# One encoder layer on one core: the first stage in an order fixed by hand, half as many sines, and Hyena's projection begun in its tail

## The chip, the cores and the metric

The kernel runs on one core of a Trainium2 chip. The metric is device time in microseconds (us) of one execution; the median of three runs is shown. A profiled execution gives the trace from which all rows below are read. The engines are TensorE (PE in the rows, its weight loads PEld), VectorE (DVE), ScalarE (ACT), GpSimd (POOL) and SyncE (SP). Transfers are issued by SyncE, by ScalarE or by GpSimd; a trailing q (SPq, ACTq) marks the issuing of a transfer.

## The reference, cut to what matters

One layer of an encoder over 2048 tokens of width 1024, in 32-bit floats. The first product's columns go to attention (8 query heads, 2 key heads and 2 value heads of 64) and to Hyena (`u`, 1536 columns):

```python
a = rms_norm(h, norm1_g[i])
q, k, v, u = jnp.split(a @ w_in[i], [512, 640, 768], axis=-1)
q = apply_axial_rope(rms_norm(q, q_norm_g[i]), *tables)
k = apply_axial_rope(rms_norm(k, k_norm_g[i]), *tables)
att = block_attention(q, k, v)                 # softmax over all 2048 keys
hy = hyena_mixer(u, ...)                       # short conv of u, then two long convolutions by FFT
```

Hyena's filters come from a small network over the 2048 positions, evaluated for all positions in both directions:

```python
z = jnp.concatenate([t, jnp.cos(ang), -jnp.sin(ang)], axis=-1)      # 2048 x 33
h = jnp.sin(freq * (z @ w1 + b1))
h = jnp.sin(freq * (h @ w2 + b2))
h = jnp.sin(freq * (h @ w3 + b3))
h = (h @ w4) * jnp.exp(-t * jnp.abs(deltas))
fwd, bwd = h[:, :, 0], h[:, :, 1]                                   # bwd enters reversed
```

Behind this come the Fourier transforms of filters and signal, the mix of both heads with an output projection, and a squared-ReLU MLP.

## The kernel before

Products of 32-bit accuracy are made from three matmuls of split operands, `high x high`, `high x low`, `low x high` (`mm3`, lines 162 to 166). Every operand is therefore split into a high part (ScalarE, a rounding copy) and a low part (VectorE, a subtraction).

**First stage** (`qkv_proj`, line 172). Sixteen tiles of 128 tokens. For each tile: load `xt`; ScalarE squares and sums it, takes a square root, scales (`xs`, lines 204, 116, 206); TensorE transposes it in eight pieces (`tp`, line 215); ScalarE and VectorE split it (`ah`, `al`, lines 217 and 218); both parts go to DRAM as `aT_d`. Then 24 matmuls of 512 columns make q and 24 of 256 columns make k and v (`qkv<-wh,ah` and its two companions). ScalarE copies and squares the result (`y`, `z`, `v`), GpSimd multiplies by gains and cosines, VectorE makes norms and the rotation, the result is split (`hl`, `kk`), transposed (`tq`, line 279), copied (`qs`, line 281) and stored. The weights `wh` and `wl` are split at the start from eight raw rows of 512 and eight of 256 columns (lines 189 to 193, raw tiles `wraw`, two buffers each).

Beside it `filter_hidden` (line 1226) goes on by a step a tile: the three sine layers, in 16 arguments of 512 columns (a matmul `fo` and seven VectorE instructions each, lines 1213 to 1219) and 16 sines on ScalarE (line 1250). Its small weights are loaded by SyncE.

In this stage a list scheduler sets the order of instructions on each engine: an instruction that is ready may go ahead of an earlier one that waits.

**Attention** (`attention`, line 445) runs 512 steps, each a score block of 128 keys by 512 queries, and begins with 22 more that make only the peaks of scores (`sc`, `top`, AHEAD = 22). Side work goes along: a generator is pumped once a step. Its first 16 steps make filter taps (`filter_taps`, `ft`, `taps`), then one step of taps alternates with six of `u_proj` (line 330), Hyena's projection: 48 column tiles (four blocks of 512 tokens by 12 tiles of 128 columns) of 24 matmuls `uo<-aT,uw` each, from the stored `aT_d` and from raw weights `uraw` that are split in the first block. What the side generator has left over at the end of attention runs off alone. The small tables `cw`, `cb` (short convolution), `dl` and `skip` are loaded by SyncE where they are used, their elements far apart in DRAM (lines 336, 339, 1294, 1302). Attention's softmax weights are `p` (line 484). The next stage begins with `fs` (line 1482).

Of the kernel before, what the change touches and what calls it, by code (L numbers as in the profile page):

```python
# [11 lines left out]
F32 = mybir.dt.float32  # L12
# [33 lines left out]
def setup(tc, ctx, a):  # L46
# [10 lines left out]
    aligned(k.cpool, 64)  # L57
# [104 lines left out]
def mm3(k, out, l_hi, l_lo, r_hi, r_lo, start, stop):  # L162
    mm = k.nc.tensor.matmul
    mm(out, l_hi, r_hi, start=start, stop=False)  # L164
    mm(out, l_hi, r_lo, start=False, stop=False)  # L165
    mm(out, l_lo, r_hi, start=False, stop=stop)  # L166


XL, FL = 1, 3


def qkv_proj(k, pa, ps, side):
# [12 lines left out]
    wh = pa.tile([P, ND, W], F32R, name="wh", bufs=1)  # L185
    wl = pa.tile([P, ND, W], F32R, name="wl", bufs=1)

    def load_w(c0, c1):
        for d in range(ND):
            raw = pa.tile([P, c1 - c0], F32, name=f"wraw{c0}", bufs=2)  # L190
            nc.sync.dma_start(out=raw[:], in_=w_in[d * P:(d + 1) * P, c0:c1])
            nc.scalar.mul(out=wh[:, d, c0:c1], in_=raw[:], mul=k.g1[:, d:d + 1])
            nc.vector.scalar_tensor_tensor(out=wl[:, d, c0:c1], in0=raw[:], scalar=k.g1[:, d:d + 1],
                                           in1=f32(wh[:, d, c0:c1]), op0=ALU.mult, op1=ALU.subtract)

    def load_x(t):
        xt = pa.tile([P, DM], F32, name="xt", bufs=2)
        nc.sync.dma_start(out=xt[:], in_=x[t * P:(t + 1) * P, :])
        return xt

    def normed(t, xt):
        xs = pa.tile([P, DM], F32, name="xs", bufs=XL + 1)
        ssq = pa.tile([P, 1], F32, name="ssq")
        nc.scalar.activation(out=xs[:], in_=xt[:], func=AF.Square, accum_out=ssq[:])
        r = rstd_from_root(k, pa, ssq[:], DM, 1, "rstd")
        nc.scalar.mul(out=xs[:], in_=xt[:], mul=r[:])
        return xs

    def turned(t, xs):
        hi = pa.tile([P, ND, P], F32R, name="ah", bufs=2)  # L210
        lo = pa.tile([P, ND, P], F32R, name="al", bufs=2)
        for d0 in range(0, ND, 4):
            tp = ps.get("tp", "tp")
            for d in range(4):
                nc.tensor.transpose(tp[:, d * P:(d + 1) * P], xs[:, (d0 + d) * P:(d0 + d + 1) * P], k.ident[:])
            c = tp[:].rearrange("p (d t) -> p d t", t=P)
            nc.scalar.copy(out=hi[:, d0:d0 + 4], in_=c)
            nc.vector.tensor_sub(out=lo[:, d0:d0 + 4], in0=c, in1=f32(hi[:, d0:d0 + 4]))
        for i, part in enumerate((hi, lo)):
            nc.sync.dma_start(out=k.aT_d[i, :, t * P:(t + 1) * P].rearrange("(d p) t -> p d t", p=P), in_=f32(part[:]))  # L220
        return hi, lo

    def project(hi, lo, c0, cw):
# [5 lines left out]
    NH = NQ + NKV  # L229

    def taken(t, oq, okv):
        y = pa.tile([P, NH, HD], F32, name="y", bufs=2)
        nc.scalar.copy(out=y[:, :NQ], in_=oq[:].rearrange("p (h e) -> p h e", e=HD))
        nc.scalar.copy(out=y[:, NQ:], in_=okv[:, :P].rearrange("p (h e) -> p h e", e=HD))
        v = pa.tile([P, NKV, HD], F32, name="v")
        nc.scalar.copy(out=v[:], in_=okv[:, P:2 * P].rearrange("p (h e) -> p h e", e=HD))
        nc.sync.dma_start(out=k.v_d[t], in_=v[:])
        z = pa.tile([P, NH, HD], F32, name="z", bufs=2)
        nc.scalar.activation(out=z[:, :NQ], in_=oq[:].rearrange("p (h e) -> p h e", e=HD), func=AF.Square)
        nc.scalar.activation(out=z[:, NQ:], in_=okv[:, :P].rearrange("p (h e) -> p h e", e=HD), func=AF.Square)  # L240
        cs = pa.tile([P, 2, HD], F32, name="cs", bufs=2)
        nc.sync.dma_start(out=cs[:], in_=a["rope"][t * P:(t + 1) * P])
        for i, s in enumerate((slice(0, NQ), slice(NQ, NH))):
            n = s.stop - s.start
            nc.gpsimd.tensor_mul(out=y[:, s], in0=y[:, s], in1=qkg[:, i:i + 1].to_broadcast([P, n, HD]))
        w = pa.tile([P, NH, HD], F32, name="w", bufs=2)
        nc.gpsimd.tensor_mul(out=w[:], in0=y[:], in1=cs[:, 0:1].to_broadcast([P, NH, HD]))
        return y, z, w, cs

    def norm_rope(t, y, z, w, cs):  # L250
        ss = pa.tile([P, NH], F32, name="ss")
        nc.vector.tensor_reduce(out=ss[:], in_=z[:], axis=AX.X, op=ALU.add)
        r = rstd_from_root(k, pa, ss[:], HD, NH, "qr")
        yv = y[:].rearrange("p h (a b e) -> p h a b e", a=2, b=2)
        zv = z[:].rearrange("p h (a b e) -> p h a b e", a=2, b=2)
        sv = cs[:, 1].rearrange("p (a b e) -> p a b e", a=2, b=2)
        for ax in range(2):
            for b in range(2):
                nc.vector.tensor_mul(out=zv[:, :, ax, b], in0=yv[:, :, ax, 1 - b],
                                     in1=sv[:, ax, b].unsqueeze(1).to_broadcast([P, NH, 16]))  # L260
        nc.vector.tensor_add(out=w[:], in0=w[:], in1=z[:])
        nc.vector.tensor_mul(out=w[:], in0=w[:], in1=r[:].unsqueeze(2).to_broadcast([P, NH, HD]))
        hl = pa.tile([P, NH, 2, HD], F32R, name="hl", bufs=FL)
        nc.scalar.copy(out=hl[:, :, 0], in_=w[:])
        nc.vector.tensor_sub(out=hl[:, :, 1], in0=w[:], in1=f32(hl[:, :, 0]))
        return hl

    def twice(hl):
        kk = pa.tile([P, NKV, 2, 2, HD], F32R, name="kk", bufs=FL - 1)
        nc.gpsimd.tensor_copy(out=kk[:, :, :, 0], in_=f32(hl[:, NQ:]))  # L270
        nc.gpsimd.tensor_copy(out=kk[:, :, 0, 1], in_=f32(hl[:, NQ:, 0]))
        nc.gpsimd.tensor_copy(out=kk[:, :, 1, 1], in_=unit[:].unsqueeze(1).to_broadcast([P, NKV, HD]))
        return hl, kk

    def finish(t, hl, kk, g):
        tp = ps.get("tq", "tq", F32R)
# [12 lines left out]
    xt, xs, aT, yz, hl = {}, {}, {}, {}, {}  # L289
    xt[0] = load_x(0)  # L290
    load_w(0, QW)
    xt[1] = load_x(1)
    load_w(QW, W)
    qkg = pa.tile([P, 2, HD], F32, name="qkg", bufs=1)
    nc.sync.dma_start(out=qkg[:, 0], in_=a["q_norm_g"].to_broadcast([P, HD]))
    nc.sync.dma_start(out=qkg[:, 1], in_=a["k_norm_g"].to_broadcast([P, HD]))
    nc.vector.tensor_scalar_mul(out=qkg[:, 0], in0=qkg[:, 0], scalar1=HD ** -0.5)
    oq = {}
    for i in range(-1 - XL, NT + FL):
        if i == 13:  # L300
            k.first = load_q(k, 0), {(0, b): load_k(k, k.early, 0, b, 4) for b in range(2)}, load_v(k, k.early, 0)
        if 1 < i + XL + 2 < NT:
            xt[i + XL + 2] = load_x(i + XL + 2)
        e = i - FL
        ending = 0 <= e < NT
        if ending:
            finish(e, *hl[e], 0)
        if 1 < i < NT:
            oq[i] = project(*aT[i], 0, QW)
        if ending:  # L310
            finish(e, *hl[e], 1)
        if 0 <= i + 1 < NT:
            aT[i + 1] = turned(i + 1, xs.pop(i + 1))
        if 0 <= i + XL + 1 < NT:
            xs[i + XL + 1] = normed(i + XL + 1, xt.pop(i + XL + 1))
        if 0 <= i + 1 < 2:
            oq[i + 1] = project(*aT[i + 1], 0, QW)
        pump(side, 1 if i > 0 else 0)
        if ending:
            finish(e, *hl.pop(e), 2)  # L320
        if 0 <= i < NT:
            okv = project(*aT.pop(i), QW, 256)
        if 0 <= i - 1 < NT:
            hl[i - 1] = twice(norm_rope(i - 1, *yz.pop(i - 1)))
# [1495 lines left out]
```

## Time and profile before

| | |
|---|---|
| median of three runs | 3129.85 us (3125.67 to 3130.92) |
| profiled execution | 3129.86 us |
| its span, first to last instruction | 3127.9 us |
| mean granted clock of TensorE | 0.980 of full speed |
| busy: TensorE, VectorE, GpSimd, ScalarE | 95%, 65%, 55%, 45% of the span |
| last product of the first stage, first `p`, next stage's first matmul | 208.0, 268.8, 1219.0 us |

Busy time counts the stretches in which an engine executes something. A granted clock of 1.00 is the upper of TensorE's two levels, 2.4 GHz, and 0.50 the lower, 1.2 GHz; matmuls overlap at their ends, so a matmul's own duration is longer than the distance to the next. Idle time of an engine names the instruction that ended it. An engine with a low share of the span can still be the one that is waited for in a stretch.

### The profile page before, as it was taken

The numbers are of one execution on the slowest core, as the hardware profiler recorded it, in microseconds if no ns is written. First come the engines' busy times: TensorE is split into PE (matmuls) and PEld (weight loads), VectorE is DVE, ScalarE is ACT, GpSimd is POOL, SyncE is SP. The second block draws the span as 40 slices with busy tenths as digits, with TensorE's granted clock in tenths as the row PEclk, the third lists the DMA queues.
The fourth block names the chain that finished last, engine by engine and source line by source line (L and its number), as shares of the span: only waits on it lengthen the run. The fifth ranks groups of instructions, "written<-read, shape, count | busy, mean of one in ns | idle before, by whom it ended". The sixth has DMA issues, their size and how long they took to land.

```text
span 3127.9 us, 40514 instructions
## 1 busy us (share of the span) xinstructions
PE 2985.5 (95%) x13400; PEld 2247.5 (72%) x13400; DVE 2047.3 (65%) x3157; ACT 1421.5 (45%) x2626; POOL 1717.1 (55%) x1395
## 2 busy tenths in 40 slices
PE   8978999999999998999999989999999899999998
PEld 6755666666666666676667768887888778888887
DVE  7987776666666654777465567777977554454455
ACT  7866655555555444444444563333333233223333
POOL 3434777777778885244555327777877553250010
PEclk9988999999999999999999999999999999999999
DMA  7758344333424525776656794445544393433454
GB/s 225 223 155 241 113 130 137 113 112 121 151 96 119 157 91 163 267 251 213 188 174 196 253 310 160 160 155 192 188 158 150 137 358 120 138 108 134 147 182 150
DMA packets 482461, 534.44 MB, mean 171 GB/s; under 512 B 49604, under 2 KB 344004, under 8 KB 475212
## 3 DMA queue, kind: packets, MB, share of 16 engines
q1 hardware_dynamic: 463708, 511.59, 50.3%
q0 software_dynamic: 4480, 14.68, 1.3%
q10 hardware_dynamic: 14064, 5.58, 0.7%
q8 instruction: 107, 1.75, 0.2%
q14 instruction: 102, 0.84, 0.1%
HBM read 326.22 MB, written 198.19 MB: 168 GB/s over the span
## 4 chain that ended last, share of the span: by engine, by line
PE 41%; DMA 3%; POOL 2%; issue 2%; ACT 1%; DVE 1%; ACTq 0%; SPq 0%; POOLq 0%; DVEq 0%
PE y L164 7%; PE y L165 7%; PE y L166 7%; PE g L166 5%; PE g L165 5%; PE g L164 5%; PE X L1451 1%; PE b L1582 1%; DMA ml<-sb 1%; PE yo L1647 1%; PE op L166 0%; PE op L164 0%; POOL r L956 0%; PE op L165 0%; ACT sb L793 0%
## 5 line engine op out<-in xcount | busy, mean ns | idle before, releaser
L489 POOL TENSOR_TENSOR sum<-sum,p 128x512 f32<-128x512 f32 x416 | 553.1, 1329 | 120.6 <-ACT p L484 94.8
L464 DVE TENSOR_REDUCE top<-sc 128x1 f32<-128x512 f32 x512 | 346.9, 686 | 252.3 <-PE sc L461 249.2
L484 ACT ACTIVATE p<-st 128x512 f32<-128x512 f32 x512 | 303.1, 597 | 302.2 <-PE st L482 285.3
L164 PE MATMUL g<-mh,wop 128*128 128x512 f32 x896 | 350.7, 391 | 5.7 <-ACT wop L922 5.4
L166 PE MATMUL g<-mh,wop 128*128 128x512 f32 x896 | 350.8, 391 | 2.4 <-DVE wop L923 2.4
L165 PE MATMUL g<-ml,wop 128*128 128x512 f32 x896 | 350.8, 392 | 2.2 <-DVE ml L933 2.2
L164 PE MATMUL y<-bh,ah 128*128 128x512 f32 x768 | 300.0, 391 | 12.4 <-ACT ah L1127 12.4
L1106 DVE TENSOR_TENSOR ah<-ar,ah 128x1024 fp32r<-128x1024 f32 x111 | 150.1, 1353 | 229.7 <-ACT ah L1105 227.2
L165 PE MATMUL y<-bh,ah 128*128 128x512 f32 x768 | 299.8, 390 | 0.0
L166 PE MATMUL y<-bh,ah 128*128 128x512 f32 x768 | 299.8, 390 | 0.0
L1105 ACT CAST ah<-ar 128x1024 fp32r<-128x1024 f32 x111 | 117.1, 1055 | 345.6 <-PE y L166 334.0
L502 PE MATMUL o<-p,vt 128*64 128x512 f32 x1024 | 234.9, 599 | 0.0
L461 PE MATMUL sc<-kt,q 128*128 128x512 f32 x512 | 208.5, 412 | 13.4 <-DVE top L464 11.6
L481 PE MATMUL st<-q,kt 128*128 128x512 f32 x512 | 214.5, 419 | 1.3 <-ACT p L484 1.2
L482 PE MATMUL st<-q,kt 128*128 128x512 f32 x512 | 203.1, 397 | 0.0
L164 PEld LDWEIGHTS g<-mh,wop 128*128 128x128 f32 x896 | 169.3, 189 | 41.8 <-ACT wop L922 6.0
L166 PEld LDWEIGHTS g<-mh,wop 128*128 128x128 f32 x896 | 169.4, 189 | 38.3 <-DVE wop L923 3.3
L165 PEld LDWEIGHTS g<-ml,wop 128*128 128x128 f32 x896 | 169.2, 189 | 38.4 <-DVE ml L933 3.3
L922 ACT CAST wop<-ws 128x512 fp32r<-128x512 f32 x128 | 79.3, 621 | 231.2 <-PE g L166 173.6
L164 PEld LDWEIGHTS y<-bh,ah 128*128 128x128 f32 x768 | 144.8, 188 | 43.0 <-ACT ah L1127 12.9
L165 PEld LDWEIGHTS y<-bh,ah 128*128 128x128 f32 x768 | 144.6, 188 | 30.4 <-DVE bh L1098 0.3
L166 PEld LDWEIGHTS y<-bh,ah 128*128 128x128 f32 x768 | 144.6, 188 | 30.1 <-DVE ah L1128 0.3
(303 smaller groups left out, 7050.4 us busy)
## 6 DMA issues: line engine op xcount, KB each, us to landing
ar<-H_d SPq DMA_DIRECT2D x109, 512.0 KB, 3.8
uw<-uw_d SPq DMA_DIRECT2D x36, 1024.0 KB, 5.0
w1raw<-in_w_mlp_in SPq DMA_DIRECT2D x64, 512.0 KB, 4.3
H_d<-r SPq DMA_DIRECT2D x96, 256.0 KB, 2.2
H_d<-s SPq DMA_DIRECT2D x96, 256.0 KB, 2.0
F_d<-F SPq DMA_DIRECT2D x34, 512.0 KB, 3.4
F<-F_d SPq DMA_DIRECT2D x34, 512.0 KB, 3.9
aT<-aT_d SPq DMA_DIRECT2D x32, 512.0 KB, 6.0
```

The costliest lines, as they stand in the source:

```text
L164: mm(out, l_hi, r_hi, start=start, stop=False)
L165: mm(out, l_hi, r_lo, start=False, stop=False)
L166: mm(out, l_lo, r_hi, start=False, stop=stop)
L461: nc.tensor.matmul(s[:], u.q[:, h], kt[u.kv, b][0][:], start=True, stop=True)
L464: k.mark_v = nc.vector.tensor_reduce(out=u.top[:, h, b:b + 1], in_=s[:], axis=AX.X, op=ALU.max, negate=True)
L481: nc.tensor.matmul(s[:], lo[:, c], u.q2[:].rearrange("p h t -> p (h t)"), start=True, stop=False)
L482: nc.tensor.matmul(s[:], hi[:, c], u.q[:].rearrange("p h t -> p (h t)"), start=False, stop=True)
L484: nc.scalar.activation(out=p[:], in_=s[:], func=AF.Exp)
L489: k.mark = nc.gpsimd.tensor_add(out=u.sum[:], in0=u.p0[:] if j == 1 else u.sum[:], in1=p[:])
L502: nc.tensor.matmul(u.o[cols], vt[j // 8][:, j % 8, u.kv], p[:], start=j < 2, stop=j > 13)
L1105: nc.scalar.copy(out=h[:, 0], in_=raw[:])
L1106: nc.vector.tensor_sub(out=h[:, 1], in0=raw[:], in1=f32(h[:, 0]))
```

## The change

1. **Order.** The whole first stage and the first steps of `u_proj` stand in a block in which TensorE, VectorE, ScalarE and GpSimd execute in the order in which the code is written (`in_order`); only SyncE's order is still the scheduler's. The loop over tiles is rewritten so that its parts stand in the order wanted. The weights' raw tiles get three buffers (q) and four (k, v).
2. **Sines.** The two halves of the 2048 positions are stacked on the partitions (before: the two directions), so that the inner layers are computed once for both directions: 8 arguments instead of 16. The second direction is the first, reversed by GpSimd copies. The frequency is divided by 2 pi once, so that an argument is three VectorE instructions and ScalarE scales by 2 pi within the sine.
3. **Hyena's projection** starts in the first stage: raw weights of column tile 0 from tile 11 on, its splits at tiles 12 to 14, its 24 matmuls between the last turns, and START = 30 more steps (column tiles 1 to 3) ahead of attention, where it was 0. The eight `aT` tiles lie in the space that `wh`, `wl` and `xt` leave, so their loads wait for the last product.
4. **Small loads.** `cw`, `cb`, `dl`, `skip`, the q and k gains, the 16 filter weights and biases and the two tiles `z` are issued by GpSimd instead of SyncE.

```diff
-    for i in range(-1 - XL, NT + FL):
+    for i in range(-3, NT + 2):
...
+        if own:
+            oq = project(i, *q_cols)
+        if 0 <= i - 1 < NT:
+            rot = rotation(i - 1)
+            next(rot)
...
+        if own:
+            okv[i] = project(i, *kv_cols)
+        if i > 0:
+            pump(side)
+        pump(u, {NT - 5: 1, NT - 4: 3, NT - 3: 3, NT - 2: 3}.get(i, 0))
+        if i == NT - 1:
+            pw_pool.__exit__(None, None, None)
+            pump(u)
...
     nc.vector.tensor_scalar(out=x[:], in0=ps, scalar1=bias, scalar2=freq, op0=ALU.add, op1=ALU.mult)
-    nc.vector.tensor_scalar(out=n[:], in0=x[:], scalar1=1.0 / (2.0 * math.pi), scalar2=MAGIC,
-                            op0=ALU.mult, op1=ALU.add)
-    nc.vector.tensor_scalar(out=n[:], in0=n[:], scalar1=MAGIC, scalar2=None, op0=ALU.subtract)
-    for c in TWO_PI:
-        nc.vector.scalar_tensor_tensor(out=x[:], in0=n[:], scalar=-c, in1=x[:], op0=ALU.mult, op1=ALU.add)
-    nc.vector.tensor_scalar(out=x[:], in0=x[:], scalar1=PI_IN, scalar2=-PI_IN, op0=ALU.min, op1=ALU.max)
+    nc.vector.tensor_scalar(out=n[:], in0=x[:], scalar1=MAGIC, scalar2=MAGIC, op0=ALU.add, op1=ALU.subtract)
+    nc.vector.tensor_sub(out=x[:], in0=x[:], in1=n[:])
...
-            nc.sync.dma_start(out=w3[h, i, j * H:(j + 1) * H], in_=a["filt_w3"][0])
+            nc.gpsimd.dma_start(out=w3[h, i, j * H:(j + 1) * H], in_=a["filt_w3"][0])
...
+    nc.vector.tensor_scalar_mul(out=fr[:], in0=fr[:], scalar1=1.0 / (2.0 * math.pi))
...
-    for b in range(4):
+    for b in range(2):
...
+        src = f32(k.hc[:, 0, max(p0, 1):p0 + 512])[:, ::-1]
+        nc.gpsimd.tensor_copy(out=k.hc[:, 1, SEQ - p0 - 511:SEQ - max(p0, 1) + 1], in_=src)
...
-START = 0
+START = 30
...
+            with sbuf(k, "uf") as k.uf:
+                k.u, k.u_tag, k.calm = u_proj(k), "qk", True
+                with sbuf(k, "p1", 2, side="right") as p1, sbuf(k, "f1", side="right") as f1:
+                    with Banks(k, "ps1", {"tp": 2, "qk": 3, "tq": 2, "fl": 1}) as k.ps, in_order(tc):
+                        qkv_proj(k, p1, k.ps, filter_hidden(k, f1, k.ps), k.u)
+                        k.calm = False
+                        pump(k.u, START)
```

What this moves is seen in each engine's order of instructions. GpSimd's, between the work on q of tile 1 and on k and v of tile 1 (`w_471` to `w_473` are the filter's weights, `fb` and `fr` its biases and frequencies; in brackets the counters that an instruction waits for); before:

```order
L245 TENSOR_TENSOR y<-y,qkg 128x512 [waits DVE_49,Activation_49]
L245 TENSOR_TENSOR y<-y,qkg 128x512 [waits Activation_49]
L245 TENSOR_TENSOR y<-y,qkg 128x128 [waits DMAHW2_49,Activation_49]
L247 TENSOR_TENSOR w<-y,cs 128x640 [waits DMAHW3_49,Pool_49]
L245 TENSOR_TENSOR y<-y,qkg 128x128 [waits Activation_49]
L271 CAST kk<-hl 128x2x64 [waits Activation_49]
```

now:

```order
L1328 DMA fr<-in_filt_freq 64x1 [waits DMASW5_49]
L1322 DMA w_471<-in_filt_w 33x64 [waits DMASW6_49]
L1323 DMA w_472<-in_filt_w 64x64 [waits DMASW7_49]
L1325 DMA w_473<-in_filt_w 64x64 [waits DMASW0_49]
L1325 DMA w_473<-in_filt_w 64x64 [waits DMASW1_49]
L1327 DMA fb<-in_filt_b 64x1 [waits DMASW2_49]
L1327 DMA fb<-in_filt_b 64x1 [waits DMASW3_49]
L1327 DMA fb<-in_filt_b 64x1 [waits DMASW4_49]
L1328 DMA fr<-in_filt_freq 64x1 [waits DMASW5_49]
L274 TENSOR_TENSOR y<-y,qkg 128x128 [waits Activation_49]
L280 TENSOR_TENSOR w<-y,cs 128x640 [waits DMAHW4_49,Pool_49]
```

These are the last nine of sixteen loads that stand between two steps of the rotation where there were none; each waits for a counter of the queue that an earlier load raises, and the work on tile 1 (`y`, `w`) follows behind them.

VectorE's, between the low parts `al` of tile 2 and the rotation of tile 1 (`ss` is the sum of squares of the heads, `qry`, `qre`, `qr` the steps to its inverse root); before, at the first rotation:

```order
L121 SCALAR_TENSOR_TENSOR rstd<-rstde,rstd 128x1 [waits DVE_49]
L252 TENSOR_REDUCE ss<-z 128x10 [waits Activation_49]
L218 TENSOR_TENSOR al<-tp,ah 128x512 [waits DMAHW4_49,Activation_49]
L218 TENSOR_TENSOR al<-tp,ah 128x512 [waits Activation_49]
L114 TENSOR_SCALAR qry<-ss 128x10 [waits DVE_49]
L259 TENSOR_TENSOR z<-y,cs 128x10x16 [waits Pool_49]
L259 TENSOR_TENSOR z<-y,cs 128x10x16
L118 RECIPROCAL qr<-qre 128x10 [waits Activation_49]
```

now:

```order
L304 TENSOR_TENSOR hl<-w,hl 128x10x64 [waits Activation_49]
L249 TENSOR_TENSOR al<-tp,ah 128x512 [waits Activation_49] x2
L1329 TENSOR_SCALAR fr<-fr 128x1 [waits DMASW5_49]
L285 TENSOR_REDUCE ss<-z 128x10 [waits Activation_49]
L118 TENSOR_SCALAR qry<-ss 128x10 [waits DVE_49]
L294 TENSOR_TENSOR z<-y,cs 128x10x32 [waits Pool_49]
L294 TENSOR_TENSOR z<-y,cs 128x10x32
L122 RECIPROCAL qr<-qre 128x10 [waits Activation_49]
```

The new row is the division of `fr`, which waits for a load that GpSimd issued.

TensorE's, behind the last product of the first stage (`hl` and `kk` are what `tq` transposes, `fo` is a product of the filter's layers, `uo` one of Hyena's projection); before:

```order
L164 MATMUL qkv<-wh,ah 128x256
L165 MATMUL qkv<-wl,ah 128x256
L166 MATMUL qkv<-wh,al 128x256
L279 MATMUL tq<-identr,hl 128x128 [waits DVE_49,Activation_49]
L279 MATMUL tq<-identr,hl 128x128 x3
L279 MATMUL tq<-identr,hl 128x128 [waits Activation_49]
L279 MATMUL tq<-identr,hl 128x128 x3
L1255 MATMUL fo<-sx,w_387 128x512 [waits DVE_49]
L279 MATMUL tq<-identr,kk 128x128 [waits Activation_49,Pool_49]
L279 MATMUL tq<-identr,kk 128x128 x3
```

now:

```order
L169 MATMUL qkv<-wl,ah 128x256
L170 MATMUL qkv<-wh,al 128x256
L316 MATMUL tq<-identr,hl 128x128 [waits DVE_49,Activation_49]
L316 MATMUL tq<-identr,hl 128x128 x3
L168 MATMUL uo<-aT,uw_2006 128x512 [waits DMAHW0_49]
L169 MATMUL uo<-aT,uw_2006 128x512
L170 MATMUL uo<-aT,uw_2006 128x512
L168 MATMUL uo<-aT,uw_2006 128x512 [waits DMAHW1_49]
L169 MATMUL uo<-aT,uw_2006 128x512
L170 MATMUL uo<-aT,uw_2006 128x512
L316 MATMUL tq<-identr,hl 128x128 [waits Activation_49]
L316 MATMUL tq<-identr,hl 128x128 x3
```

Between the turns of the last two tiles now stand matmuls of the projection, each group of three waiting for the load of one `aT` tile; the filter's products stand earlier.

## Rows read from the trace of the kernel before

**Rows 1.** Page, busy time of each engine, share of the span, instructions.
```profile
PE 2985.5 (95%) x13400; PEld 2247.5 (72%) x13400; DVE 2047.3 (65%) x3157; ACT 1421.5 (45%) x2626; POOL 1717.1 (55%) x1395
```

**Rows 2.** Stretches: length; busy time by engine; granted clock; share of transfer engines; GB/s.
```profile
core 0: us, PE busy (x) PEld busy (x) DVE busy (x) ACT busy (x) POOL busy (x), PEclk, DMA share, GB/s
13.00:31.50 18.50, 17.93 (x84) 14.16 (x83) 10.07 (x29) 14.31 (x27) 2.59 (x2) 1.00 0.93 284
31.50:208.00 176.50, 165.25 (x992) 137.61 (x990) 162.21 (x362) 134.99 (x257) 74.91 (x84) 0.98 0.68 202
208.00:270.00 62.00, 33.34 (x90) 18.84 (x90) 45.24 (x95) 34.26 (x72) 7.10 (x9) 0.61 0.74 181
270.00:544.00 274.00, 260.33 (x1106) 171.49 (x1104) 204.83 (x345) 162.52 (x342) 198.09 (x150) 0.98 0.46 145
544.00:1194.00 650.00, 649.46 (x2876) 431.64 (x2875) 400.41 (x613) 337.01 (x603) 526.19 (x399) 1.00 0.37 119
1194.00:1219.00 25.00, 23.08 (x104) 16.48 (x103) 3.84 (x11) 4.22 (x7) 5.24 (x5) 1.00 0.59 143
```

**Rows 3.** Time line of TensorE: start, length, instruction, count, idle time before.
```profile
26.07 0.39 PE L164 MATMUL qkv<-wh,ah 128*128 128x512 f32 x1
26.30 0.39 PE L165 MATMUL qkv<-wl,ah 128*128 128x512 f32 x1
...
31.31 1.03 PE L215 MATMUL tp<-ident,xs 128*128 128x128 f32 x8
...
203.90 1.09 PE L1255 MATMUL fo<-sx,w 128*128 128x512 f32 x2
...
207.95 0.28 PE L166 MATMUL qkv<-wh,al 128*128 128x256 f32 x1
...
228.44 1.61 PE L461 MATMUL sc<-kt,q 128*128 128x512 f32 x3
232.81 0.79 PE L461 MATMUL sc<-kt,q 128*128 128x512 f32 x1 [2.76 <-DVE top L464]
237.05 1.48 PE L461 MATMUL sc<-kt,q 128*128 128x512 f32 x2 [3.44 <-DVE top L464]
...
247.79 1.39 PE L461 MATMUL sc<-kt,q 128*128 128x512 f32 x2 [5.08 <-DVE top L464]
...
1219.03 1.05 PE L1482 MATMUL fs<-table,e 128*128 128x128 f32 x8
```

**Rows 4.** Groups by form on VectorE, 0 to 230 us: busy, mean ns.
```profile
L1218 DVE SCALAR_TENSOR_TENSOR sx<-sn,sx 128x512 f32<-128x512 f32 x32 | 28.1, 878 | 0.3
```

**Rows 5.** Transfers issued in the first 275 us: count, size, us to landing.
```profile
wraw<-in_w_in SPq DMA_DIRECT2D x8, 128.0 KB, 3.5
...
uraw<-in_w_in SPq DMA_DIRECT2D x2, 512.0 KB, 8.3
...
w<-in_filt_w SPq DMA_DIRECT2D x6, 16.0 KB, 3.3
```

**Rows 6.** Time line of ScalarE.
```profile
16.28 1.06 ACT L204 ACTIVATE xs<-xt 128x1024 f32<-128x1024 f32 x1 [1.97 <-DMA xt<-in_x]
...
18.96 1.14 ACT L206 ACTIVATE xs<-xt,rstd 128x1024 f32<-128x1024 f32 x1
...
22.86 2.33 ACT L192 ACTIVATE wh<-wraw,g 128x512 fp32r<-128x512 f32 x4
...
268.76 0.60 ACT L484 ACTIVATE p<-st 128x512 f32<-128x512 f32 x1 [0.99 <-PE st L482]
```

**Rows 7.** Line 800's instructions: GpSimd issuing a transfer, ns min/median/max.
```profile
L800 POOL DMA_DIRECT2D ml<-sb x20: 536/536/538, 1778.4 to 1828.8; - x20
```

**Rows 8.** Time line of SyncE's queue.
```profile
231.00 3.45 SPq L1302 DMA_DIRECT2D skip<-in_hy_skip_d  x1
...
241.95 6.44 SPq L339 DMA_DIRECT2D cb<-in_hy_conv_b  x1
```

**Rows 9.** Time line of GpSimd.
```profile
26.72 1.29 POOL L245 TENSOR_TENSOR y<-y,qkg 128x512 f32<-128x512 f32 x1 [24.56 <-ACT y L233]
```

More of the change, by code (lines that the diff above doesn't have):

```diff
@@ L227, in project @@
         return o
[L229 to L248, printed above, removed]
@@ L268, in twice, with heads @@
[L268 to L276, printed above, removed]
+    def heads(o, n):
+        return o[:, :n * HD].rearrange("p (h e) -> p h e", e=HD)
@@ new lines, in qkv_proj @@
+    xt, xs, rs, aT, y, z, w, cs, hl, kk, tq, okv = ({} for _ in range(12))
+    q_cols, kv_cols = (0, QW), (QW, W)
+    load_x(0)
+    for d in range(4):
+        load_w(d, *q_cols)
+    load_x(1)
+    for d in range(4, ND):
+        load_w(d, *q_cols)
+    for d in range(4):
+        load_w(d, *kv_cols)
+    load_x(2)
+    for d in range(4, ND):
+        load_w(d, *kv_cols)
+    nc.gpsimd.dma_start(out=qkg[:, 0], in_=a["q_norm_g"].to_broadcast([P, HD]))
+    nc.gpsimd.dma_start(out=qkg[:, 1], in_=a["k_norm_g"].to_broadcast([P, HD]))
@@ new lines, in qkv_proj @@
+    k.qkg = qkg
+    small_tables(k)
+    ahead = {-2: range(4), -1: range(4, ND)}
+    for i in range(-3, NT + 2):
+        norms = rot = iter(())
+        own, mine = 0 <= i < NT, 0 <= i - 2 < NT
+        tail = i >= NT
+        if 2 < i + 5 < NT:
+            load_x(i + 5)
+        if i == NT - 3:
+            k.first = load_q(k, 0), {(0, b): load_k(k, k.early, 0, b, 4) for b in range(2)}, load_v(k, k.early, 0)
+        if mine:
+            turn(i - 2, 0)
+        if tail:
+            pump(u, 2)
+        if 0 <= i - 1 < NT:
+            taken(i - 1, okv.pop(i - 1), 1)
+        if mine:
+            stored(i - 2, 0)
+        if own:
[3 more added lines that the diff above has]
+            next(rot)
+        if 0 <= i + 2 < NT:
+            scaled(i + 2)
+        if i == -2:
+            turned(0)
+            turned_low(0)
+        for d in ahead.get(i, ()):
+            split_w(d, *q_cols)
+        pump(rot)
+        if 0 <= i + 3 < NT:
+            norms = squared(i + 3)
+            pump(norms, 2)
+        pump(rot)
+        pump(norms)
+        if mine:
+            turn(i - 2, 1)
+        if tail:
+            pump(u, 2)
+        pump(rot)
+        if mine:
+            stored(i - 2, 1)
+        if 0 < i + 1 < NT:
+            turned(i + 1)
+        pump(rot)
+        if 0 < i + 1 < NT:
+            turned_low(i + 1)
+        if i == 0:
+            for d in range(ND):
+                split_w(d, *kv_cols)
+        if mine:
+            turn(i - 2, 2)
+        if own:
+            taken(i, oq, 0)
+        if mine:
+            stored(i - 2, 2)
+        if own:
+            okv[i] = project(i, *kv_cols)
+            del aT[i]
+        if i > 0:
[4 more added lines that the diff above has]
+            pump(u)
```

289 lines of the change are left out of this document (156 added, 133 removed).

## The prediction

> **What bounds the kernel now.** I read the busy shares first, then stretches of the first 1219 us, then groups of instructions, then the time lines at the seams. TensorE is busy in 2985.5 of 3127.9 us [rows 1], so only its 142 us of gaps, its slow-clock stretches and whatever work is taken off it can pay. The stretches show where the change can reach [rows 2]. From 31.5 to 208 us (the products of the token tiles) TensorE is busy 165.25 of 176.5 us, so 11.25 us are gaps, and VectorE is busy 162.21: the two bind together. From 208 to 270 TensorE is busy only 33.3 of 62 us, at a mean granted clock of 0.61, that is, for most of it at the lower of its two levels (1.2 of 2.4 GHz). From 270 to 544 it is busy 260.3 of 274, and from 544 to 1194 it is full (649.46 of 650) at clock 1.00. From 1194 to 1219 the last products of Hyena's projection run with almost nothing of attention beside them. Behind 1219 the code is the same, so I take that part over at its present length and predict one number: when the stage that now starts at 1219.03 [rows 3] will start.
>
> **Sines.** Before there were 16 arguments, now 8, each with one `fo` product of two records, which keep TensorE busy for 1.09 us [rows 3], some 1.0 beyond what overlaps. Thirteen of the 16 fall before 208 us: 13 us of the 165.25 go and 8 come back. On VectorE seven instructions an argument become three; the two dearest, of 0.88 us each [rows 4], are among those that go, so 32 x 0.88 = 28 us at least leave an engine that was busy for 162 of 176.5. VectorE stops being a bound in that stretch, and its gaps no longer explain TensorE's. Fewer table loads on ScalarE lay beside TensorE's products; I give them nothing.
>
> **The start.** Before, TensorE takes products of q0, q1 and kv0 as weights arrive: at 31.31 us all 72 are through and the next transposes begin [rows 3]. In the fixed order it runs q0, then kv0, then q1, each complete. kv0's last four weight rows are loaded into the buffers of its first four, so SyncE's issue waits until VectorE has split those; such a load lands after 3.5 us [rows 5]. The split stands on ScalarE behind four squares, three scalings, two pairs of `ah` and eight parts of q: by its rows 4 x 1.25, 3 x 1.14 and, at 0.58 each (four in 2.33 us), twelve more, 15.4 us [rows 6], from 5 us on without any wait for a load. So kv's splits begin at 21 to 23 and its last at 31 to 34. I get q0 at 25 to 27, kv0 at 37 to 39, and q1 5.5 us later (24 x 0.23, the distance from one wide product to the next [rows 3]), or up to 49 where the slow clock comes in: all 72 at 45, against 31.3. That is a loss of 13.7, with 10 and 17.7 as its ends.
>
> **The rest of the first stage.** TensorE's work behind those 72 is 165.25 - 13 + 8 = 160.2 us. To it come waits that the fixed order makes.
> (a) VectorE's `fr<-fr` stands between the low parts of tile 2 and the sum of squares of tile 1, and needs the sixteenth of the filter loads, which POOL issues behind `y` of q1. POOL issues a load in 0.536 us [rows 7], each of the last eight waits for the one eight earlier, and SyncE's loads of this kind landed after 3.3 us [rows 5]: 8.6 us if no wait bites, plus one landing, 11.9. Everything behind it on VectorE waits, and through it ScalarE and, once q2 and kv1 are through, TensorE. I take 9, ends 4 and 20 (two landings of some 6 us beside the issues).
> (b) `z` is one more POOL load for each half of the filter's positions, and TensorE's `fo` waits for it in its queue: an issue and a landing, 0.5 + 3.3, I take 4, ends 0 and 6.
> (c) Three batches of sines stand on ScalarE ahead of the copy of kv, and the next layer's products wait for them in TensorE's queue. No row shows such a wait; its ends are nothing and, three times, two products as long as a pair of records (1.09 us [rows 3]), 6.5. I take 4.
> (d) Of today's 11.25 us of gaps I keep 2, at the turns, ends 0 and 3.
> Together 19, ends 6 and 35. The last product then ends at 45 + 160.2 + 19 = 224 (before 208).
>
> The four small tables (4608 + 1536 + 2048 + 1024 elements of four bytes) go to POOL's queue as well. Bounds: 4 x 0.54 = 2.2 us [rows 7]; or, at the 6.44 us for which the issue of the 1536 elements of `cb` holds SyncE's queue [rows 8], 4.2 ns each, 39 us. POOL has no tile work before 26.72 us [rows 9] and none that TensorE waits for before about 40, so the upper end costs 0 to 3 us; I take 0. SyncE gains: `skip` (3.45 us) and `cb` no longer hold it at 231 and 242 [rows 8], where the loads of `aT` stood behind.
>
> The Trainium skill (DMA: Bandwidth & Descriptors, "Anatomy of one DMA — SWDGE (gpsimd) path") fits a POOL-issued transfer by a fixed 2.0 us plus its bytes. The trace shows 0.536 us of POOL for one and no small load among them; if the 2.0 us were paid one after the other, sixteen would take 32 us, and (a) would be some 29 instead of 9.
>
> **The tail.** Before, from the last product (207.95 [rows 3]) to the first weight `p` of attention (268.76 [rows 6]) pass 60.7 us. Now the pools' space puts the eight `aT` loads (8 x 512 KB) behind the last product: 14.8 us at the 284 GB/s that the start reached [rows 2]. Column tile 0 of the projection goes along with their landing. Tile 1 runs at a clock that I take from the present tail, 5.5 / 0.61 = 9 us, or 10.3 wholly at the lower level; tile 2 at full clock, 5.5; tile 3 waits for its raw weights, whose load stands behind the store of tile 1 and lands after 8.3 us [rows 5], so it ends about 40 us after the last product. Then come the score peaks of the first 22 steps and the filter's taps. Before, from the first score (228.44) to `p` pass 40.3 us, of which 2.8 + 3.4 + 5.1 are the longest waits [rows 3], behind SyncE's tables and the weights `w4`; 29 stay, set by VectorE. 40 + 29 = 69: `p` at 293. In exchange four column tiles and 0.6 of a fifth are done, 4.6 x 5.5 = 25.5 us of TensorE.
>
> **Attention.** Before, from the first `p` to the next stage 1219.03 - 268.76 = 950.3 us. TensorE is full there, so the 25.5 us go away whole. Of the 13.7 us of gaps between 270 and 544, where the first block's twelve column tiles are also split, 4.6 twelfths go, 5.2. The last dozen attention steps run without projection beside them and wait for their exponentials; I add 2.3 (ends 0 and 6). 950.3 - 25.5 - 5.2 + 2.3 = 921.9. No flush is left: 521 steps of side work meet 538 places for them.
>
> **Sum.** 224 + 69 + 921.9 = 1214.9, against 1219.0: a gain of 4.1 us. The profiled execution took 3129.86 us (1.96 beyond its span), the median of three is 3129.85, so I forecast 3126. What can be told from no change is about 0.2%, 6.3 us.
>
> **Rivals.**
> A. The fixed order hides its loads: the start costs 10 us only and the waits 6 in all, as they would if VectorE's `fr` finds its load landed. Then the last product ends at 41.5 + 160.2 + 6 = 208, as before, and the projection's tiles show whole: the next stage at 1199, a time of 3110. For it speaks that VectorE is relieved and that the 11.25 us of gaps were partly its own; against it that VectorE and ScalarE now take every wait in one queue, where before other work went ahead.
> B. POOL's queue decides: VectorE stands at `fr` for 20 us and the start is at its upper end. 49 + 160.2 + 32 = 241, 17 later than forecast, so 3143, slower than before. It decides from the point where `fr` lands more than 15 us behind `y` of q1. For it: no small POOL load stands in the trace, and engines in order pass a stall on to each other; against it: q2 and kv1, over 8 us of TensorE, do not need what stands behind `fr`. By the skill's 2.0 us in a row the end would be 3143 or later.
> C. The tiles moved into the tail buy nothing: their loads and splits hold up the peaks, `p` comes 80 instead of 69 us after the last product. Then 3137, just slower.
>
> **How the numbers follow.** Forecast 0.46 (its own range 3119 to 3134, of which two fifths lie below 3123.6), A 0.24, B 0.18, C 0.12. Faster by over 0.2%: 0.24 + 0.19 = 0.43. Slower by over 0.2%: 0.18 of B and 0.09 of C, 0.27. Within 0.2% the rest, 0.30. The range takes in B and C to their centres and A beyond its own: 3106 to 3143.
>
> **What would show it.** The last product of the first stage at 224 (208 in A, 241 in B); VectorE idle ahead of `fr<-fr` for over 4 and under 20 us; TensorE idle between 13 and 50 us for some 13 us more than now; the first score some 40 us and `p` some 69 us behind the last product; no long `skip` and `cb` rows on SyncE; no stretch of projection alone between attention's end and the next stage. The forecast is wrong in kind if the stretch from the first `p` to the next stage does not shrink to about 922 us.

## The result, and the profile after

The changed kernel takes 3136.14 us (median of 9 runs, 3132.61 to 3142.10) against 3129.85 us (9 runs): ratio 1.0027, 95% interval 1.0017 to 1.0037. It is slower by 6.3 us by the medians, by 8.4 by the means, which the ratio is nearer to; the forecast was 3126, faster by 4. The profiled execution took 3142.1 us, at the upper end of the runs, so its trace is read for where time goes, and differences in time are taken from the medians.

Stretches of the changed kernel, in the columns of [rows 2]: the start up to the 72nd product, the rest of the first stage, the tail up to the first `p`, attention in three pieces.

```profile
13.00:53.80 40.80, 26.36 (x81) 18.66 (x81) 19.48 (x51) 20.90 (x41) 3.30 (x3) 0.75 0.63 186
53.80:241.40 187.60, 162.30 (x994) 138.52 (x992) 122.88 (x274) 110.99 (x237) 71.26 (x110) 0.94 0.66 192
241.40:320.00 78.60, 51.70 (x180) 35.47 (x180) 44.52 (x112) 42.60 (x104) 5.23 (x9) 0.80 0.92 279
320.00:590.00 270.00, 265.73 (x1166) 175.73 (x1165) 203.73 (x328) 161.11 (x313) 207.10 (x157) 0.99 0.41 136
590.00:1221.00 631.00, 629.64 (x2794) 416.60 (x2794) 376.65 (x591) 329.11 (x588) 515.93 (x391) 1.00 0.35 114
1221.00:1231.00 10.00, 4.44 (x20) 2.67 (x17) 0.26 (x2) 1.50 (x3) 7.47 (x6) 0.82 0.55 55
```

The 72 products end at 53.8 us where they ended at 31.3, at a granted clock of 0.75. The rest of the first stage takes 187.6 us although its work fell to 162.3 (against 165.25 of 176.5 in [rows 2]): 25 us of gaps instead of 11, at clock 0.94. The tail, from the last product at 241.20 to `p`, takes 78.8 us against 60.8, and attention, from `p` at 319.98 to the next stage at 1230.66, 910.7 instead of 950.3. The next stage starts 11.6 us later than in [rows 3].

What TensorE and VectorE waited for in the rest of the stage (us in total, times, longest):

```profile
PE fo L1339 <- DMA z<-in_zT: 17.7, 2, 14.0
PE tq L316 <- ACT ah L243: 4.4, 4, 1.5
PE fo L1339 <- ACT sx L1334: 3.2, 2, 2.2
```

```profile
DVE sx L1299 <- PE fo L1339: 29.3, 8, 7.4
DVE fr L1329 <- DMA fr<-in_filt_freq: 13.1, 1, 13.1
```

and GpSimd's time line there, with VectorE's and TensorE's at its end:

```profile
56.23 1.30 POOL L274 TENSOR_TENSOR y<-y,qkg 128x512 f32<-128x512 f32 x1 [0.74 <-ACT y L272]
...
58.01 0.58 POOL L1322 DMA_DIRECT2D w<-in_filt_w  x1
...
65.83 1.55 POOL L1327 DMA_DIRECT2D fb<-in_filt_b  x3 [1.37 <-DMA fb<-in_filt_b]
67.37 0.52 POOL L1328 DMA_DIRECT2D fr<-in_filt_freq  x1
...
75.47 0.40 POOL L306 CAST kk<-hl 128x256 fp32r<-128x256 f32 x1 [5.48 <-DVE hl L304]
...
76.57 1.26 POOL L274 TENSOR_TENSOR y<-y,qkg 128x512 f32<-128x512 f32 x1 [0.23 <-ACT y L272]
77.78 0.57 POOL L1345 DMA_DIRECT2D z<-in_zT  x1
```

```profile
69.57 0.15 DVE L1329 TENSOR_SCALAR fr<-fr 128x1 f32<-128x1 f32 x1 [13.09 <-DMA fr<-in_filt_freq]
...
74.58 0.83 DVE L304 TENSOR_TENSOR hl<-w,hl 128x640 fp32r<-128x640 f32 x1
```

```profile
82.18 2.04 PE L1339 MATMUL fo<-z,w 66*128 66x512 f32 x2 [13.96 <-DMA z<-in_zT]
```

It is one chain through the queues of GpSimd, VectorE, GpSimd again and TensorE. VectorE's largest wait in total, 29.3 us in eight times, is for the filter products; its longest, 7.4 us, stands behind this chain. The sixteen loads hold GpSimd from 58.0 to 67.9 us; VectorE stands 13.1 us at `fr<-fr`; the rotation of tile 1 ends with `hl` at 74.58; GpSimd's `kk` at 75.47 waits for that, `y` of q2 behind it, and only then, at 77.78, is `z` issued. TensorE's first filter product stands ahead of q3 and waits 14.0 us for `z`. The three waits of TensorE above, 25.3 us, are all its gaps in this stretch. GpSimd had sat idle from 7.7 to 46.2 us.

### The profile page after: what moved, and what is told of

It is laid out like the page before. It is cut to its first block, busy times and chain, and to the rows that moved or that the text cites. A ratio compares the mean times of both kernels' runs of the same rounds, so it can differ in the third digit from the quotient of the medians.

```text
span 3140.3 us, 40401 instructions
## 1 busy us (share of the span) xinstructions
PE 2976.8 (95%) x13384; PEld 2245.9 (72%) x13384; DVE 1984.8 (63%) x3050; ACT 1394.4 (44%) x2593; POOL 1713.8 (55%) x1424
## 4 chain that ended last, share of the span: by engine, by line
PE 77%; DMA 4%; DVE 4%; issue 3%; POOL 2%; ACT 2%; SPq 0%; POOLq 0%; ACTq 0%; DVEq 0%
PE o L589 7%; PE y L169 6%; PE y L168 6%; PE y L170 6%; PE g L170 5%; PE g L169 5%; PE g L168 5%; PE st L568 4%; PE X L1536 4%; PE st L569 4%; PE sc L548 3%; PE uo L168 3%; PE uo L169 3%; PE uo L170 3%; PE b L1667 2%
## 5 line engine op out<-in xcount | busy, mean ns | idle before, releaser
L1192 DVE TENSOR_TENSOR ah<-ar,ah 128x1024 fp32r<-128x1024 f32 x111 | 149.7, 1350 | 231.5 <-ACT ah L1191 231.5
L548 PE MATMUL sc<-kt,q 128*128 128x512 f32 x512 | 202.0, 398 | 5.0 <-DVE top L551 4.5
L168 PEld LDWEIGHTS y<-bh,ah 128*128 128x128 f32 x768 | 144.6, 188 | 42.9 <-ACT ah L1213 12.9
L168 PE MATMUL uo<-aT,uw 128*128 128x512 f32 x384 | 154.0, 401 | 19.7 <-ACT uw L438 9.6
L170 PEld LDWEIGHTS y<-bh,ah 128*128 128x128 f32 x768 | 144.4, 188 | 30.5 <-DVE ah L1214 0.3
```

What stands on the lines that cost most here:

```text
L170: return mm(out, l_lo, r_hi, start=False, stop=stop)
L548: nc.tensor.matmul(s[:], u.q[:, h], kt[u.kv, b][0][:], start=True, stop=True)
L1192: nc.vector.tensor_sub(out=h[:, 1], in0=raw[:], in1=f32(h[:, 0]))
```

## The experiments

Medians, with the ratio to the kernel before as it was timed beside each of the four groups of experiments (its medians there: 3131.48, 3132.44, 3131.56, 3131.69). Differences to the changed kernel are given by the medians; those by the ratios are 2 to 5 us larger.

**Filter loads early.** The step of `filter_hidden` that loads, now with both tiles `z`, is taken before the loop over tiles.
```diff
+    for b in range(2):
+        zs.append(f1.tile([66, 512], F32, name="z", bufs=2))
+        nc.gpsimd.dma_start(out=zs[b][:], in_=a["zT"][:, b * 512:(b + 1) * 512])
+    yield
...
     k.qkg = qkg
+    pump(side)
     small_tables(k)
```


> The sixteen filter loads and the two z tiles are issued by GpSimd at the start (it sits idle from 8 to 46 us), instead of behind the gains on q of tile 1. If the stall at GpSimd's queue is what made the stage late (13.1 us of VectorE before the division of fr, 17.7 us of TensorE before the first filter products, and a slow clock behind them), the last product of the first stage comes at 241 - 20 = 221 (215 to 226), and the time falls by some 20 us to 3116 (3110 to 3122). Rival: the filter loads only fill gaps that the fixed order would have anyway, the last product stays within 5 us of 241, the time within 5 us of 3136. Rival: the loads crowd the start, whose 72 products then come later than 53.7.

3119.48 us, ratio 0.9963 (0.9950 to 0.9976). The last product comes at 218.3 instead of 241.2. The stretch from the 72nd product has 8.6 us of gaps instead of 25.3, and its work takes 157.9 us instead of 162.3, at clock 0.99:

```profile
13.00:52.00 39.00, 28.21 (x80) 19.20 (x81) 18.74 (x49) 20.29 (x41) 10.99 (x13) 1.00 0.70 179
52.00:218.50 166.50, 157.86 (x994) 136.31 (x992) 126.09 (x275) 111.12 (x238) 61.28 (x89) 0.99 0.74 214
218.50:296.40 77.90, 52.16 (x180) 35.99 (x180) 44.52 (x112) 42.53 (x104) 5.21 (x9) 0.80 0.91 281
```

The waits at the loads and the slow clock behind them cost 17 us by the medians (20 by the ratios). The start did not suffer (72 products at 51.9, at a clock of 1.00), so up to 2 of the 17 us are the start's.

**Three rows split first,** ahead of the square root of tile 0.
```diff
+            if i == -3:
+                for d in range(3):
+                    split_w(d, *q_cols)
-    ahead = {-2: range(4), -1: range(4, ND)}
+    ahead = {-2: range(3, 6), -1: range(6, ND)}
```


> The first three raw weight rows are split ahead of the square root of tile 0, instead of behind its transposes, so that their three buffers come free some 7 us earlier and the other five rows are loaded earlier. If the start is bound by these buffers, the 72 products come at 53.7 - 7 = 47 (44 to 50) and the time falls by 5 to 9 us to 3129. Rival: the start is bound by what the transfer queues carry (tokens ahead, a raw tile of the projection, small tables), then the 72 products stay at 52 to 55 and the time within 3 us of 3136.

3135.04 us, ratio 1.0013 (1.0003 to 1.0022). The 72 products come at 47.7 in the trace, as the first theory has it, and the last product at 234.5: TensorE waits 17.6 us for `z` as before, so the 6 us are kept to the end of the stage. Yet the median is only 1 us below the changed kernel's (4 by the ratios), where 5 to 9 were expected. What takes the rest is not shown.

**Tables late.**
```diff
-    small_tables(k)
...
+        if i == 4:
+            small_tables(k)
```


> The four small tables (9216 elements of four bytes) are issued by GpSimd in tile 4 instead of at the start. If their small elements hold up the weights' loads at the start, the 72 products come 4 to 8 us earlier than at 53.7 and the time falls by as much. If they are hidden, as I forecast, nothing changes there (within 2 us), and GpSimd's 5 us of issue may show in tile 4: time 3134 to 3140.

3135.12 us, ratio 1.0014 (1.0005 to 1.0024): again the 72 products (49.2) and the last product (236.5) come sooner, and the median is 1 us less (4 by the ratios). In the changed kernel the four take 5 us of GpSimd's issue, inside my bounds of 2.2 and 39.

**START = 0.**
```diff
-START = 30
+START = 0
```


> START = 0 instead of 30: column tiles 1 to 3 of the projection go into attention's side work; column tile 0 stays in the first stage's tail. The first score should come some 32 us earlier (264 instead of 296), p some 30 us earlier, and attention from first p to the next stage takes 16.6 us of TensorE and some gaps more, about 930 instead of 911. If the tiles in the tail buy less than they cost, as rival C says, the time falls by 5 to 12 us; if they pay as forecast, it rises by 3 to 10 us.

3136.40 us, ratio 1.0021 (1.0011 to 1.0030): no difference. `p` comes 60.4 us behind the last product instead of 78.8, and the next stage starts 16 us sooner in the trace; but the span's rest grows by 13.6 us, 9.7 of them one wait at that stage's beginning. The projection's last product comes right ahead of that stage here (1214.0, against 1200.3 with START = 30). What the tiles in the tail gain or lose is made up there.

**The three edits together, with START 30 and 20.**

> Three edits together: the filter loads and z at the start, the first three weight rows split ahead of the square root, the four small tables in tile 4. If the stalls are of different places and add up, the last product comes at 218 - 4 to 6 = 213 and the time at 3113 to 3116, against 3119.5 with the early loads alone. Rival: the edits of the start share one limit (the transfers ahead of the weights), then 3118 to 3120 as with the loads alone.

> The same with START = 20: column tile 3, whose split waited behind the filter weights w4 for 8 us with TensorE idle, goes into attention. If that wait is lost time, the first score comes 15 us earlier than in the combined kernel (10 us of it the tile's own matmuls at a partly low clock), attention takes some 6 us more, and the time falls by 3 to 8 us. Rival: a tile fewer in the tail is a tile more in attention, and nothing changes, as with START = 0 (within 3 us).

3107.71 us, 0.9922 (0.9905 to 0.9939), and 3107.86, 0.9923 (0.9908 to 0.9938). With the loads out of the way the two edits of the start, worth 1 us each alone by the medians (4 by the ratios), are worth 12 together (72 products at 44.2, last product at 210.7, both some 8 us sooner than with the loads alone). Both theories of the first were too small; how the 12 divide between the two edits is not shown. Column tile 3 is no loss in the tail.

**No fixed order.**
```diff
-  with Banks(k, "ps1", {"tp": 2, "qk": 3, "tq": 2, "fl": 1}) as k.ps, in_order(tc):
+  with Banks(k, "ps1", {"tp": 2, "qk": 3, "tq": 2, "fl": 1}) as k.ps:
```


> The changed kernel without the fixed order: the list scheduler sets all engines' order again. If the loads on GpSimd's queue cost only because the order lets nothing pass, TensorE waits for them no more (the waits of 13 and 18 us go), and the last product comes at 241 - 20 to 30 = 211 to 221, the time at 3106 to 3118. Rival: the loads are slow by themselves, or the scheduler does worse with the new code: 3130 and more.

3095.13 us, ratio 0.9886 (0.9871 to 0.9901), faster than both kernels and 41 us below the changed one by the medians (44 by the ratios). The last product comes at 204.4, with 72 products at 36.4, and `p` 70.4 us behind it. Stretches, and GpSimd's time line:

```profile
13.00:36.50 23.50, 19.07 (x88) 15.60 (x87) 11.59 (x37) 16.44 (x35) 8.66 (x16) 1.00 1.02 288
36.50:204.50 168.00, 157.05 (x995) 134.53 (x994) 128.49 (x284) 125.61 (x255) 76.50 (x95) 1.00 0.79 224
204.50:274.80 70.30, 53.48 (x182) 36.59 (x181) 43.05 (x110) 40.51 (x99) 3.29 (x4) 0.81 0.94 298
```

```profile
8.78 0.55 POOL L1322 DMA_DIRECT2D w<-in_filt_w  x1
...
22.30 0.52 POOL L1328 DMA_DIRECT2D fr<-in_filt_freq  x1
22.81 1.05 POOL L1345 DMA_DIRECT2D z<-in_zT  x2
31.14 1.37 POOL L274 TENSOR_TENSOR y<-y,qkg 128x512 f32<-128x512 f32 x1 [7.28 <-ACT y L272]
```

The scheduler itself puts the same loads into GpSimd's idle time, 8.8 to 23.9 us, ahead of `y` of q0. Nothing waits for them any more. Of the 41 us the early loads gave 17 and the two edits of the start 12. Some 13 remain between the three edits together and this run; in the traces they lie in the start (72 products at 36.4 instead of 44.2) and in the tail (70.4 us instead of 76.5), and no run takes these two apart.

**GpSimd's loads in the kernel before.** All `nc.sync.dma_start` of `filter_hidden` become `nc.gpsimd.dma_start`.

> The kernel before with its sixteen filter loads and four z tiles issued by GpSimd instead of SyncE, nothing else. If loads on GpSimd hurt only in a fixed order, the time stays within 4 us of 3130. If GpSimd's queue is slow by itself, the sines start later and the last product comes 8 to 20 us later, the time at 3138 to 3150.

3131.51 us, ratio 0.9997 (0.9988 to 1.0007): these loads cost nothing by being GpSimd's. They cost where the order lets nothing pass.

**The new sines alone** in the kernel before: `sin_argument`, `filter_hidden` and its table of positions as in the change, with `nc.sync` loads.

> The kernel before with the change's sines alone (8 arguments instead of 16, three VectorE instructions each, the second direction by reversed copies); loads stay on SyncE, the scheduler sets the order. TensorE loses 8 us of products, VectorE 50 us. Forecast's reading: VectorE and TensorE bound the stretch together, so most of the 8 us and part of the 11 us of gaps go: the last product at 196 to 202 instead of 208, the tail 5 us shorter as no sines are left for it, time 3112 to 3122. Rival: something else sets the pace (transfers, the rotation), the last product stays at 206 to 209 and the time within 5 us of 3131.

3100.98 us, ratio 0.9899 (0.9882 to 0.9915): 30.6 us, more than I gave them in any theory. The last product comes at 201.8, and the tail falls from 60.8 to 39.1 us. The tail in two pieces, last product to first score and first score to `p`, with the new sines and then in the kernel before:

```profile
201.80:212.00 10.20, 4.71 (x39) 3.94 (x38) 6.12 (x13) 6.11 (x14) 4.69 (x9) 0.81 0.70 213
212.00:240.90 28.90, 21.69 (x52) 12.04 (x52) 21.87 (x51) 17.13 (x38) 0.00 (x0) 0.74 0.93 253
```

```profile
208.00:228.40 20.40, 8.88 (x42) 5.30 (x42) 20.01 (x37) 13.16 (x25) 7.10 (x9) 0.68 0.35 107
228.40:268.80 40.40, 23.26 (x47) 12.62 (x47) 24.27 (x57) 19.90 (x44) 0.00 (x0) 0.58 0.93 220
```

Before, VectorE was busy for 20.0 of the 20.4 us ahead of the first score: the last two filter products lay behind the last product, and their arguments and the splits of `hc` stood among the rotation of the last tile. The weights `w4` came behind the last sine. With the new sines that chain ends in the first stage (last sine and first load of `w4`, new sines first):

```profile
140.67 0.64 ACT L1248 ACTIVATE sx<-sx 128x512 f32<-128x512 f32 x1
...
150.15 0.55 ACTq L1294 DMA_DIRECT2D w<-in_filt_w  x1
```

```profile
228.91 0.63 ACT L1250 ACTIVATE sx<-sx 128x512 f32<-128x512 f32 x1 [0.62 <-DVE sx L1219]
229.58 0.53 ACTq L1290 DMA_DIRECT2D w<-in_filt_w  x1
```

The loads went along: `dl` is issued at 143.8 us instead of 230.5, `skip` at 152.5 instead of 231.0. So the run does not part VectorE's work in the tail from the loads that came behind it: some 10 us went ahead of the first score, 11 behind it.

**Without the fixed order: the three edits, and START = 0.**

> The changed kernel without the fixed order, with the three edits of the combined kernel (loads of filter and z at the start, three rows split first, tables in tile 4). If the scheduler already walks around all these waits, the time stays at 3095 (3091 to 3099). If the start still holds some of them (72 products at 36 us, before 31), it falls to 3086 to 3091.

> Without the fixed order and with START = 0: column tiles 1 to 3 go back into attention. With the fixed order START made no difference (3136.4 against 3136.1). If the tail's tiles fill time that TensorE would idle, the time rises here by 5 to 15 us to 3100 to 3110; if they only hold up the peaks, it stays within 4 us of 3095 or falls.

3101.28 us, 0.9899 (0.9884 to 0.9914): the three edits by hand are worse than what the scheduler does by itself (72 products at 40.3 instead of 36.4). And 3097.86, 0.9886 (0.9871 to 0.9901): START makes no difference here either.

**128 bytes of shift, and swapped pools,** in the kernel before and in the one with the new sines.
```diff
-    aligned(k.cpool, 64)
+    aligned(k.cpool, 192)
```
```diff
-  with sbuf(k, "at") as at, sbuf(k, "up") as up:
+  with sbuf(k, "up") as up, sbuf(k, "at") as at:
```


> The kernel before with one gap tile 128 bytes longer, so that everything behind it in the on-chip memory lies 128 bytes further (attention's `kt`, `p` and the projection's `aT` then at multiples of 256 bytes, as in the changed kernel; before, 128 beyond). In attention two wide products follow each other after 231.6 ns before and 228.8 ns in the changed kernel. If the addresses make that difference, attention's pace goes to about 229 ns and the stretch from the first p to the next stage from 950 to 938 us; later stages may move too. If something else makes it (the side work, the other engines), the pace stays at 231 to 232 and the stretch at 950.

> The kernel before with attention's two pools opened in the other order, so that the projection's tiles lie at 59 to 125 KB and keys, weights and sums above, as in the changed kernel. If the place of the tiles sets the pace in attention, wide products follow after 229 instead of 231.6 ns and the stretch from first p to the next stage takes 938 instead of 950 us; the time falls by some 10 us to 3121, if the tail does not suffer from other space being waited for. If not, the pace stays at 231 to 232 and the time within 5 us of 3131.

> The same swap in the kernel with the new sines alone (3101.0). If places set the pace: attention 935 instead of 947, time 3087 to 3092, which would be the best so far. If not: 3097 to 3105.

3132.79 us, 0.9999 (0.9990 to 1.0008); 3133.08, 1.0005 (0.9995 to 1.0016); 3107.04, 0.9918 (0.9902 to 0.9935). The pace stays at 231 to 232 ns in all three: neither the shift nor the place of the pools makes the faster pace of the changed kernel. With the new sines the swap costs 6 us; in the trace they lie behind attention and were not followed.

**The order fixed only from tile 2 on** (`k.order` is the context that `in_order` makes).
```diff
+        if i == 2:
+            k.order.__enter__()
```


> The changed kernel with the order fixed only from tile 2 on; the scheduler orders what stands ahead of it. By the milestones the start should give back 17 of the 41 us (72 products at 36 instead of 54), and the stall at GpSimd's filter loads, which lies behind tile 1, should stay: 3136 - 17 = 3119 (3115 to 3123). Rival: a start that is ahead of the loads only waits longer for them, and 3126 to 3134 come out; or the loads are ordered early by the scheduler, and 3100 to 3110.

3140.41 us, ratio 1.0025 (1.0015 to 1.0036): inconclusive. The 72 products still come at 52.4 and the loads stand where they stood; the instructions ahead of the fixed part kept the written order too, so the share of the start was not separated.

**The new sines with START = 30** in the old code (`START = 0` to `START = 30`).

> The kernel before with the new sines and START = 30: 16 steps of taps and some 12 of the projection run ahead of attention. If early side work only moves what TensorE would do later, the time stays within 3 us of 3101. If it fills the tail's idle TensorE, it falls to 3094 to 3098; if it holds up the peaks without filling gaps, it rises to 3104 to 3112.

3109.03 us, ratio 0.9927 (0.9912 to 0.9941), 8 us worse than the sines alone: `p` comes 47.2 us behind the last product instead of 39.1. Early side work held up the peaks, as the third theory has it.

## Why the prediction was wrong

By the terms of its sum: the last product was to come at 224 and came at 241.2, the tail took 78.8 us instead of 69, attention 910.7 instead of 921.9. The next stage starts 15.8 us later than forecast. The terms that failed are prices of the new order and the new tail, each put too low: the start, the waits behind it, and the tail up to the first score.

- **The fixed order** costs 41 us by the run without it, more than the 37 us that the rest of the change gains. "The rest of the first stage" failed in (a) and (b), 9 and 4 us of TensorE, which I added up as two separate waits. VectorE stood 13.1 us for (a), as forecast by kind, but what reached TensorE came through (b). I priced `z` at an issue and a landing; its issue stood behind `kk` and `y` in GpSimd's queue, and these behind (a). TensorE waited 17.7 us, and its clock fell to 0.81 between 54 and 100 us, which stretched its work by 4 us against the run with early loads. Taken away, (a), (b) and the clock give 17 us (shown). (c), 4 us, was near, 3.2 measured; the gaps kept in (d), 2 us, were 4.4.
- **Rival B** named this end, 241, and the last product came at 241.2, by luck: what it decided by, `fr` more than 15 us behind `y` of q1, did not occur (`y` ended at 57.5, `fr` at 69.6), and its start of 49 was too early by 5 and its rest too long by as much.
- **The sines** were mis-sized the other way, so this error did not make the forecast too fast; it hid part of the order's price. I gave them 5 us of TensorE and, in (d), 9 us of gaps. Alone they bring 30.6 us. The gaps did not go with VectorE's relief: alone the sines leave 10.3 us of them up to the last product (TensorE busy 160.0 of 170.3 us), so (d) failed. The gain lies in the tail, whose waits I put down to SyncE's tables and `w4` [rows 3, 8]. It takes 39.1 us with the new sines, though the tables are still SyncE's: the loads came late because the filter's arguments ended late, and ahead of the first score VectorE itself was the bound, for which I had no term.
- The Trainium skill (DMA: Bandwidth & Descriptors, "Anatomy of one DMA — SWDGE (gpsimd) path") gives a GpSimd-issued transfer a fixed 2.0 us plus its bytes. That these follow one after the other, which the prediction weighed, is not what the trace shows: sixteen were issued in 9.9 us. As the time of a single transfer the trace is near it: 2.2 us passed from the last load's issue (67.37) to the instruction that waited for it (69.57).
- **The start,** 45 us, its worst end 49, came at 53.8. I had the splits on ScalarE run "without any wait for a load"; they waited 14.0 us for loads, since a row is loaded only into a buffer that an earlier split has left, and other loads stand between on SyncE's queue:

```profile
13.68 1.95 ACT L214 ACTIVATE wh<-wraw,g 128x512 fp32r<-128x512 f32 x3
23.72 0.72 ACT L214 ACTIVATE wh<-wraw,g 128x512 fp32r<-128x512 f32 x1 [8.09 <-DMA wraw<-in_w_in]
...
32.62 0.72 ACT L214 ACTIVATE wh<-wraw,g 128x512 fp32r<-128x512 f32 x1 [2.86 <-DMA wraw<-in_w_in]
```

  Earlier splits (47.7) and later tables (49.2) each bring the 72 products forward.

- **The tail,** 69 us, took 78.8. The first score came 54.8 and not 40 us behind the last product. Two thirds of this were lost before column tile 3: the first `aT` let TensorE go 9.3 us behind the last product, tile 0 ended at 22.2 instead of 14.8 us behind it, and tile 2 at 39.6 instead of 29.3. Then tile 3 waited for its split, and the split stood on ScalarE behind a cast that waited for `w4`, not for its own raw weights:

```profile
250.54 0.79 PE L168 MATMUL uo<-aT,uw 128*128 128x512 f32 x1 [7.33 <-DMA aT<-aT_d]
...
280.44 0.39 PE L170 MATMUL uo<-aT,uw 128*128 128x512 f32 x1
288.88 0.79 PE L168 MATMUL uo<-aT,uw 128*128 128x512 f32 x1 [8.05 <-ACT uw L438]
```

```profile
287.90 0.62 ACT L1381 CAST w4h<-w 128x512 fp32r<-128x512 f32 x1 [5.90 <-DMA w<-in_filt_w]
288.43 2.44 ACT L438 ACTIVATE uw<-uraw,g 128x128 fp32r<-128x128 f32 x8
```

  From there to `p` passed 24 us, where I had 29.
- **Attention,** 921.9 us, took 910.7: right by kind, as 4.5 column tiles lie ahead of `p` (4.6 forecast) and no projection is left over at its end. Some 7 of the 11 us more go with a pace that I had not expected (below), the rest was not traced. That it is a gain when nothing is left over was half an error: with START = 0 the projection runs up to the next stage, which starts sooner in the trace, and the time is the same.
- **Rival C,** that the tiles in the tail buy nothing, holds for column tiles 1 to 3 by both runs with START = 0. Its 80 us from last product to `p` were 78.8; that its time, 3137, is near the measured one is luck, as it had the last product at 224.
- That the tables cost nothing on GpSimd is not shown. Alone in tile 4 they change the median by 1 us, but the 72 products come 4.6 us sooner, and with the loads early their part in the 12 us was not separated.
- Slips in the working that decide nothing: the low ends of (a) to (d) add up to 4 and not 6; 14 of the 16 filter products, not 13, fell before the last product; an argument had six VectorE instructions before, not seven.

## What to carry to other kernels

An order fixed by hand makes every wait a wait for all that stands behind it, on each engine in turn: before fixing one, put each load where its engine is idle, and follow a load's issue back through its own engine's queue, not only its landing. Test the parts of a change apart: here one part brought 31 us and another lost 41. And where the waits of a tail name a transfer, ask what had to end before it could be issued: here it was an engine's leftover work.

## What the runs showed of the hardware that was not expected

In attention one wide product follows another after 231.5 ns on average in the kernel before (600 to 1100 us, distances of 221 to 245 ns) and after 228.7 ns in the changed kernel, with the same products and a granted clock of 1.00 in both; with START = 0 and without the fixed order it is 228.8 and 228.6. The commonest distance is 232 ns before and 227 ns after. In the first stage (60 to 200 us) it is the other way round: 228.5 before, 232.7 after. Over the some 2500 such distances in attention that is 7 us. Two shifts of the tiles did not change it, nor did the new sines alone or START = 30 in the old code (231.5 in both). The cause stays open.
